# Attention value products that leave PSUM in one copy, with their halves added through DRAM, and forget gates computed with tokens on partitions

## The chip, the cores and the metric

The kernel runs on one core of a Trainium2 chip. A core has a matrix engine (TensorE, PE in the profile), three engines for elementwise work (VectorE or DVE, ScalarE or ACT, GpSimd or POOL), a queue that issues transfers (SyncE or SP) and 16 DMA engines that carry them. Each engine takes its instructions in the order of the program and waits on semaphores for the others. The metric is the device time of one execution in microseconds, the median of several runs.

## The reference

One layer of an encoder, everything in float32, for 1024 tokens of width 1024. Cut to the part that the change touches:

```python
h = rmsnorm(x, g_mix_pre)
proj = h @ w_in                       # fq fk fv | f_logit (8 columns) | cq ck cv
f_logit = proj[..., 1536:1544] + b_fgt
y_fox = forgetting_attention(fq, fk, fv, f_logit)   # 8 heads of 64
y_chk = chunked_relpos_attention(cq, ck, cv, rel_bias)  # 8 heads of 64
y = concat([rmsnorm(y_fox, g_fox_out), rmsnorm(y_chk, g_chk_out)])
x = x + rmsnorm(y @ w_out, g_mix_post)

def forgetting_attention(q, k, v, f_logit):
    logf = log_sigmoid(f_logit)
    c = cumsum(logf, axis=1)          # over the tokens, one row for each head
    logits = q @ k.T / 8 + c[query] - c[key]      # causal
    return softmax(logits) @ v
```

After that come cross-attention into 256 memory tokens (`w_mq`, `w_mk`, `w_mv`, `w_mo`) and a squared-ReLU MLP of width 4096, each between two rmsnorms and added to `x`.

## The kernel before

**Products in three parts.** TensorE multiplies in a rounded 32-bit form. To keep float32 accuracy each operand is split into a high part (a rounded copy, made by ScalarE) and a low part (the rest, made by a subtraction on VectorE or GpSimd), and each product is three matmuls into one PSUM bank: high by high, high by low, low by high (`mm3`, lines 193 to 195).

**Stages.** First the value products of four heads of each kind and the normed input are computed (up to about 57 us). Then follows the attention phase (`attention_phase`), then a second run for the output projection, cross-attention and the first half of what follows (`flow.run` a second time), then the MLP, whose order is written out by hand.

**A planner sets the order.** In the attention phase and the second run the program is written by a small planner (`Flow`). It walks a clock of its own. Generators yield steps for TensorE with a cost and a condition; at each point the first generator whose condition holds emits its step, in the order in which they are listed: value products (`value_steps`), transposes of the probabilities (`turn_steps`), scores (`score_steps`), side work such as the gates and the transposes of values and memory (`side_steps`), the inverse rms (`rstd_steps`) and at the end the projections that fill the gaps (`filler_steps`: queries, keys and values of later heads, then the memory products `mk` and `mv`). Work for the other engines is put into lists with an engine, a time from which it can run and a cost: `flow.put("V", ...)` for VectorE, `"S"` for ScalarE, `"G"` for GpSimd, `"D"` and `flow.load` for transfers on SP. Buffers are counted by tokens (`free`). `pumps` are asked at each step whether a transfer or a split can be started: weights (`stock.pump`), biases (`biases.pump`), the normed outputs of the heads (`outputs.pump`). What comes out is a fixed order on each engine.

**The heads.** There are 16 heads, taken in pairs `n` = 0 to 7 in the order of `ORDER`: two pairs of chunked heads, four pairs of forgetting heads, two pairs of chunked heads. A unit is one head and 256 queries. For a unit, scores go into PSUM, VectorE adds the bias and takes the minimum, ScalarE takes the exponential, GpSimd scales by the inverse sum, TensorE transposes the probabilities (`ptr`, line 711), ScalarE and VectorE split them (`phl`, lines 720 and 717), and TensorE multiplies them by the values (`pv`, line 754). The score matmuls (`sc`, `sf`, lines 638 and 639) need the queries `qs` and the doubled keys `kd`, `kl`, whose second half is put in place by SP transfers (line 849).

**How a unit's product leaves.** The stationary operand holds high and low values side by side, so the bank `pv` has 128 partitions: for one head the high product on 64 of them and the low product on the other 64, and each has two halves of 256 columns, from the high and the low probabilities. The result is the sum of all four. `leave` (in `value_steps`) does it in three operations and a store:

```python
flow.put("S", flow.end, 0.6, lambda: nc.scalar.activation(o2[own], pv[oth, :, :, ::step], AF.Copy), both)
# both: VectorE adds the other 64 partitions of the bank (frees the bank),
#       GpSimd adds the two halves, SP stores 64 x 256 to od[kcol][g // 2]
```

`Outputs` later loads `od` (line 1045), scales and splits it for the output projection, and sums its squares; `rstd_steps` makes the inverse rms with four small matmuls for each half of the tokens (`ssh`, line 1059). `rstd_steps(0)` (forgetting heads, both halves) is a stream of the attention phase, `rstd_steps(1)` (chunked heads) one of the second run.

**The forget gates.** The value products of the first four forgetting heads carry eight further columns, the gate logits of all eight, which ScalarE copies into `fcol` (tokens on partitions, lines 350 and 355). `forget_gates` transposes them to [8, 1024] (eight transposes, `ftr`, line 521), adds the offset, computes log-sigmoid in ten operations on eight partitions (lines 526 to 537, with two loads of ScalarE's function table), takes the running sum with a scan, and stores it to `cd` (line 538), from which each forgetting head's bias is loaded (line 576).

Of the kernel before, what the change touches and what calls it, by code (L numbers as in the profile page):

```python
# [22 lines left out]
P = 128  # L23
S = 1024
D = 1024
KC = D // P
TB = S // P
HT = 512
# [27 lines left out]
class Flow:  # L56
# [79 lines left out]
def build(ctx, tc, nc, out, t):  # L136
# [151 lines left out]
    fcol = p1.tile([P, TB, 8], F32, tag="o2", bufs=2, name="fcol")  # L288
# [52 lines left out]
    def value_leave(g, kb, ps):  # L341
# [12 lines left out]
        if g == 0:  # L354
# [8 lines left out]
            dict(s=2, tr=2, pv=2, mm=2, sp=1, p=2, klo=4, bias=2, raw=2, w=0, u4=6,  # L363
                 q=4, mp=4, pt=1, xt=2, wq=0).items()}
    seen = {}

# [146 lines left out]

    def forget_gates():

        z, e, l, u = [p1.tile([8, S], F32, tag="sp", bufs=5, name=f"f{n}") for n in "zelu"]
        parts = []
        for g in range(2):
            tr = mm_tile([8, 4, P], f"ftr{g}", "tr")
            for j in range(4):  # L520
                nc.tensor.transpose(tr[:, j, :], fcol[:, g * 4 + j, :], ident)
            parts.append(("V", 0.75, lambda g=g, tr=tr: nc.vector.tensor_scalar(
                z[:, g * HT:(g + 1) * HT], tr.rearrange("p a b -> p (a b)"), bfgt, None, op0=ALU.add)))

        parts += [
            ("V", 0.7, lambda: nc.vector.tensor_scalar(l, z, -1.0, None, op0=ALU.mult)),
            ("V", 1.2, lambda: nc.vector.tensor_tensor(l, l, z, op=ALU.min)),
            ("S", 1.1, lambda: nc.scalar.activation(e, l, AF.Exp)),
            ("V", 0.7, lambda: nc.vector.tensor_scalar(u, e, 1.0, None, op0=ALU.add)),
            ("S", 2.4, lambda: nc.scalar.activation(l, u, AF.Ln)),  # L530
            ("V", 1.3, lambda: nc.vector.scalar_tensor_tensor(e, u, 1.0, e, op0=ALU.subtract, op1=ALU.subtract)),
            ("S", 2.4, lambda: nc.scalar.activation(u, l, AF.Exp, scale=-1.0)),
            ("V", 1.2, lambda: nc.vector.tensor_tensor(e, e, u, op=ALU.mult)),
            ("V", 1.2, lambda: nc.vector.tensor_sub(e, e, l)),
            ("V", 1.3, lambda: nc.vector.scalar_tensor_tensor(e, z, 0.0, e, op0=ALU.min, op1=ALU.add)),
            ("V", 0.9, lambda: nc.vector.memset(u, 0.0)),
            ("V", 2.3, lambda: nc.vector.tensor_tensor_scan(l, e, u, 0.0, op0=ALU.add, op1=ALU.add)),
            ("D", 0.55, lambda: nc.sync.dma_start(cd, l))]

        def done(at):  # L540
            seen["gates"] = at
            for _ in range(4):
                free["sp"].give(at)

        for _ in range(2):
            free["tr"].take()
        flow.chain(flow.end, parts[:2], lambda at: [free["tr"].give(at) for _ in range(2)] and
                   flow.chain(at, parts[2:], done))
# [177 lines left out]
    def value_steps():  # L726
        landed = [all_of(("od", k), 32) for k in range(2)]
        for n, a, g in units:
            kind, pr = ORDER[n]
            h = pr * 2 + a  # L730
            own, oth = HALVES[a]
# [25 lines left out]
            def leave(pv=pv, kind=kind, nm=f"{n}{a}{g}", own=own, oth=oth, kcol=kcol, g=g, step=1 if kind == "f" else -1):  # L757
                o2 = p1.tile([P, 2, 2, P], F32, tag="o2", bufs=2, name=f"o2{nm}")

                def store(end):  # L760
                    flow.load(end, lambda: nc.sync.dma_start(
                        od[kcol][g // 2][own, (g % 2) * 256:(g % 2) * 256 + 256],
                        o2[own, 0].rearrange("p a b -> p (a b)")), landed["fc".index(kind)], 2.2)

                def both(at):
                    flow.put("V", at, 0.7, lambda: nc.vector.tensor_add(  # L766
                        o2[own], pv[own, :, :, ::step], o2[own]), lambda end: (
                        free["pv"].give(end), flow.put("G", end, 0.8, lambda: nc.gpsimd.tensor_add(  # L768
                            o2[own, 0], o2[own, 0], o2[own, 1]), store)))

                flow.put("S", flow.end, 0.6, lambda: nc.scalar.activation(o2[own], pv[oth, :, :, ::step], AF.Copy), both)  # L771
# [89 lines left out]
    def side_steps():  # L861

        yield 0.87, lambda: flow.now > 2.5 and free["tr"].ready(2)
# [128 lines left out]

    class Outputs:
# [56 lines left out]
    def rstd_steps(g):  # L1050

        for th in range(2):
            yield 0.5, lambda: there(("sq", th, g)) and free["pv"].ready()
            free["pv"].take()
            sq = parts[th, g][2]
            rs = parts["rs", th, g] = small.tile([P, 4], F32, tag="rs4", bufs=4, name=f"rs{th}{g}")
            ps = mm_tile([P, 4], f"ssh{th}{g}", "pv")
            for b in range(4):
                nc.tensor.matmul(ps[:, b:b + 1], sq[:, b * P:(b + 1) * P], o512, start=True, stop=True)
# [547 lines left out]

    stock = Stock()
    with tc.manual_schedule():
# [117 lines left out]
        nc.sync.dma_start(bfgt, t["b_fgt"])  # L1727
# [684 lines left out]
def _layout(i):  # L2412
# [10 lines left out]
    def parts(w, ranges):  # L2423
# [16 lines left out]
        "b_fgt": a(i["b_fgt"].reshape(8, 1)),  # L2440
# [26 lines left out]
```

## Time and profile before

| What | us |
|---|---|
| median of 3 runs | 1462.85 (1462.04 to 1463.18) |
| span of the profiled execution | 1459.5 |
| TensorE busy in it | 1447.7 (99%) |
| VectorE, ScalarE, GpSimd busy | 996.0, 820.7, 421.0 |

The profiled execution is told by its span, from its first to its last instruction; the time of a run has some 3 us more around it. In the page, a busy TensorE is one with a matmul in flight, and matmuls overlap, so a short pause is seen in the distance between two starts rather than as idle time. Lines such as `L766` are lines of the kernel, and names such as `o<-pv` are the tile written and the tiles read, with buffer numbers left out.

### The profile page before, as it was taken

How to read it: one execution, taken by the hardware profiler on the slowest of the kernel's cores; microseconds unless marked ns; L12 is line 12 of the kernel's file. 1: busy time of each engine (PE TensorE's matmuls, PEld its weight loads, DVE VectorE, ACT ScalarE, POOL GpSimd, SP SyncE). 2: the span in 40 equal slices, each digit the busy share in tenths (PEclk: the TensorE clock that was granted, in tenths of full speed). 3: DMA queues.
4: the chain of work that ended last, by engine and by line, in shares of the span. 5: the costliest groups of instructions: out<-in, count | busy, mean ns of one | idle time of the engine just before them, and what ended most of it. 6: DMA issues, size and time to landing. Idle time of an engine off the chain costs nothing.

```text
span 1459.5 us, 21037 instructions
## 1 busy us (share of the span) xinstructions
PE 1447.7 (99%) x7265; PEld 1222.2 (84%) x7265; DVE 996.0 (68%) x1704; ACT 820.7 (56%) x1437; POOL 421.0 (29%) x520
## 2 busy tenths in 40 slices
PE   9999999999999999999999999999999999999998
PEld 8988888888889888888788888888888888888886
DVE  6777777767668847976873687765555666655576
ACT  6567677766677836555653465545555543444442
POOL 1245456555455301521332414343322000000021
PEclk9999999999999999999999999999999999999999
DMA  7132324321325584552541637754444785445565
GB/s 276 49 95 72 83 67 140 86 82 46 95 58 161 174 314 173 187 179 86 181 138 44 200 132 260 258 196 159 159 151 161 286 318 185 140 149 190 186 246 202
DMA packets 88987, 232.17 MB, mean 159 GB/s; under 512 B 10649, under 2 KB 14753, under 8 KB 88881
## 3 DMA queue, kind: packets, MB, share of 16 engines
q1 hardware_dynamic: 88736, 230.57, 47.6%
q8 instruction: 57, 0.93, 0.3%
q14 instruction: 50, 0.40, 0.1%
q10 hardware_dynamic: 144, 0.26, 0.1%
HBM read 167.30 MB, written 55.11 MB: 152 GB/s over the span
## 4 chain that ended last, share of the span: by engine, by line
PE 96%; DVE 2%; DMA 1%; ACT 1%; issue 0%; SPq 0%; DVEq 0%; ACTq 0%
PE pv L754 4%; PE fx L194 4%; PE fx L193 4%; PE fx L195 4%; PE ptr L711 4%; PE px L194 3%; PE fy L193 3%; PE px L195 3%; PE fy L195 3%; PE px L193 3%; PE fy L194 3%; PE mq L195 2%; PE q L193 2%; PE q L195 2%; PE q L194 2%; PE yw L193 2%
## 5 line engine op out<-in xcount | busy, mean ns | idle before, releaser
L717 DVE TENSOR_TENSOR phl<-ptr,phl 128x512 fp32r<-128x512 f32 (+1 forms) x152 | 92.5, 616 | 31.5 <-ACT phl L720 30.5
L2163 ACT ACTIVATE whif<-ra 128x1024 fp32r<-128x1024 f32 x37 | 39.2, 1061 | 130.3 <-PE fy L194 62.6
L2165 DVE TENSOR_TENSOR wlof<-ra,whif 128x1024 fp32r<-128x1024 f32 x37 | 45.3, 1225 | 91.7 <-ACT whif L2163 91.7
L720 ACT ACTIVATE phl<-ptr 128x512 fp32r<-128x512 f32 (+1 forms) x152 | 79.8, 540 | 40.3 <-PE ptr L711 38.5
L2285 POOL TENSOR_SCALAR rf<-sf 128x1 f32<-128x1 f32 x7 | 7.9, 1130 | 321.7 <-ACT jf L2266 321.4
L754 PE MATMUL pv<-phl,vs 128*128 128x512 f32 (+1 forms) x304 | 85.2, 366 | 0.2 <-DVE phl L717 0.2
L193 PE MATMUL fx<-vhif,whif 128*128 128x512 f32 x168 | 65.4, 389 | 0.0
L195 PE MATMUL fx<-vhif,wlof 128*128 128x512 f32 x168 | 65.4, 389 | 0.0
L194 PE MATMUL fx<-vlof,whif 128*128 128x512 f32 x168 | 65.4, 389 | 0.0
L754 PEld LDWEIGHTS pv<-phl,vs 128*128 128x128 f32 x304 | 55.2, 188 | 11.0 <-DVE phl L717 0.7
L2050 POOL TENSOR_TENSOR sc<-wf,wf 128x512 f32<-128x512 f32 x14 | 23.1, 1652 | 141.1 <-DMA wf<-in_w_ff 122.6
L768 POOL TENSOR_TENSOR o<-o 64x256 f32<-64x256 f32 x64 | 47.8, 747 | 53.1 <-DVE o L766 29.0
L193 PE MATMUL k<-hT_hi,whik 128*128 128x512 f32 x128 | 53.6, 419 | 0.0
L766 DVE TENSOR_TENSOR o<-pv,o 64x512 f32<-64x512 f32 x64 | 44.0, 688 | 13.5 <-ACT o L771 12.1
L193 PE MATMUL q<-hT_hi,whiq 128*128 128x512 f32 x128 | 51.6, 403 | 0.0
L193 PE MATMUL mq<-h2T_hi,whimq 128*128 128x512 f32 x128 | 51.4, 401 | 0.0
L195 PE MATMUL mq<-h2T_hi,wlomq 128*128 128x512 f32 x128 | 50.2, 392 | 0.2 <-DVE wlomq L455 0.2
L195 PE MATMUL k<-hT_hi,wlok 128*128 128x512 f32 x128 | 50.3, 393 | 0.0
L194 PE MATMUL k<-hT_lo,whik 128*128 128x512 f32 x128 | 50.3, 393 | 0.0
L195 PE MATMUL q<-hT_hi,wloq 128*128 128x512 f32 x128 | 50.2, 392 | 0.0
L194 PE MATMUL q<-hT_lo,whiq 128*128 128x512 f32 x128 | 50.2, 392 | 0.0
L194 PE MATMUL mq<-h2T_lo,whimq 128*128 128x512 f32 x128 | 50.1, 392 | 0.1
(696 smaller groups left out, 5014.5 us busy)
## 6 DMA issues: line engine op xcount, KB each, us to landing
ra<-gd SPq DMA_DIRECT2D x56, 512.0 KB, 3.8
wg<-in_w_ff SPq DMA_DIRECT2D x56, 512.0 KB, 5.6
wf<-in_w_ff SPq DMA_DIRECT2D x38, 512.0 KB, 3.9
gd<-s SPq DMA_DIRECT2D x48, 256.0 KB, 2.1
wrawmq<-in_w_mq SPq DMA_DIRECT2D x16, 512.0 KB, 4.3
gd<-u SPq DMA_DIRECT2D x32, 256.0 KB, 2.2
gd<-g SPq DMA_DIRECT2D x25, 256.0 KB, 2.2
wrawq<-in_w_qk SPq DMA_DIRECT2D x8, 512.0 KB, 4.4
```

Of the source, the lines that this page charges most:

```text
L193: nc.tensor.matmul(ps, lh, rh, start=start, stop=False, skip_group_check=more)
L194: nc.tensor.matmul(ps, lh, rl, start=False, stop=False, skip_group_check=more)
L195: nc.tensor.matmul(ps, ll, rh, start=False, stop=stop, skip_group_check=more)
L711: nc.tensor.transpose(tr[:, m, :], sp[:, k * P:(k + 1) * P], ident)
L717: flow.put("V", at, 0.7, lambda: nc.vector.tensor_sub(pl[:, live, :], tr[:, live, :], f(ph[:, live, :])), done)
L720: flow.put("S", flow.end, 0.6, lambda ph=ph, tr=tr, live=live: nc.scalar.activation(ph[:, live, :], tr[:, live, :], AF.Copy), split)
L754: nc.tensor.matmul(pv[:, :, qs_, :], v, hl[:, :, hs, :], start=c == 0 and turn == 0, stop=last)
L766: flow.put("V", at, 0.7, lambda: nc.vector.tensor_add(o2[own], pv[own, :, :, ::step], o2[own]), lambda end: (free["pv"].give(end), flow.pu ...
L768: free["pv"].give(end), flow.put("G", end, 0.8, lambda: nc.gpsimd.tensor_add(o2[own, 0], o2[own, 0], o2[own, 1]), store)))
L2050: eng.tensor_sub(sc[:, k1], r0[:, k0], r1[:, k0])
L2163: nc.scalar.activation(ah, ra, AF.Copy)
L2165: nc.vector.tensor_sub(al, ra, f(ah))
```

## The change

Three things.

1. **Value products.** ScalarE copies the whole bank, all 128 partitions, in one operation, and the bank is free. GpSimd adds the two halves of 256 columns on 128 partitions. SP stores 128 x 256 to a new array in DRAM, `oh`, which for a pair of heads holds four blocks of 64 rows: high and low of the first head, low and high of the second. When the four units of a pair and half of the tokens have landed, a new pump, `fold`, loads `oh` twice, with the blocks 0 and 3 in one half of a tile and 1 and 2 in the other, adds the halves on VectorE or GpSimd (whichever the planner's lists have free sooner, `pick`), and stores the sum to `od`. `Outputs` then goes on as before. The value steps no longer use VectorE.
2. **Forget gates.** The log-sigmoid is computed on `fcol` itself, [128, 8, 8], by `gate_columns` at the start of the attention phase. The eight transposes come after it; ScalarE copies their result out of PSUM, and only the scan and the store stay on [8, 1024]. The offset `b_fgt` is loaded once for all partitions. Two of the four [8, 1024] tiles are gone, so scores start with five free buffers (`sp`) instead of one, and `side_steps` waits for two of them.
3. **Inverse rms.** The second half of `rstd_steps(0)` moves from the attention phase to the second run, ahead of `rstd_steps(1)`.

```diff
+    def behind(self, eng, at):
+        return max(self.free[eng], at) + sum(i[3] for i in self.waiting[eng])
+
+    def pick(self, at, cv, cg, call, then=None, level=0):
+
+        if self.behind("V", at) + cv + 2 < self.behind("G", at) + cg:
+            self.put("V", at, cv, lambda: call(True), then, level)
+        else:
+            self.put("G", at, cg, lambda: call(False), then, level)
...
-    bfgt = const.tile([8, 1], F32, name="bfgt")
+    bfgt = const.tile([P, 8], F32, name="bfgt")
+    gate = [const.tile([P, TB, 8], F32, name=f"gate{k}") for k in "zelu"]
...
+    oh = [[dr.tile([2 * P, HT], F32, name=f"oh{k}_{h}") for h in range(2)] for k in range(KC)]
...
-            dict(s=2, tr=2, pv=2, mm=2, sp=1, p=2, klo=4, bias=2, raw=2, w=0, u4=6,
+            dict(s=2, tr=2, pv=2, mm=2, sp=5, p=2, klo=4, bias=2, raw=2, w=0, u4=6,
...
+    def gate_columns():
+
+        z, e, l, u = gate
+        b = bfgt[:, None, :].to_broadcast([P, TB, 8])
+        flow.chain(0.0, [
+            ("V", 0.17, lambda: nc.vector.tensor_tensor(z, z, b, op=ALU.add)),
+            ("V", 0.15, lambda: nc.vector.tensor_scalar(l, z, -1.0, None, op0=ALU.mult)),
+            ("V", 0.17, lambda: nc.vector.tensor_tensor(l, l, z, op=ALU.min)),
+            ("S", 0.3, lambda: nc.scalar.activation(e, l, AF.Exp)),
+            ("V", 0.15, lambda: nc.vector.tensor_scalar(u, e, 1.0, None, op0=ALU.add)),
+            ("S", 1.6, lambda: nc.scalar.activation(l, u, AF.Ln)),
+            ("V", 0.17, lambda: nc.vector.scalar_tensor_tensor(e, u, 1.0, e, op0=ALU.subtract, op1=ALU.subtract)),
+            ("S", 1.6, lambda: nc.scalar.activation(u, l, AF.Exp, scale=-1.0)),
+            ("V", 0.17, lambda: nc.vector.tensor_tensor(e, e, u, op=ALU.mult)),
+            ("V", 0.17, lambda: nc.vector.tensor_sub(e, e, l)),
+            ("V", 0.17, lambda: nc.vector.scalar_tensor_tensor(e, z, 0.0, e, op0=ALU.min, op1=ALU.add))], mark("gate"), 1)
+
     def forget_gates():
 
-        z, e, l, u = [p1.tile([8, S], F32, tag="sp", bufs=5, name=f"f{n}") for n in "zelu"]
+        l, u = [p1.tile([8, S], F32, tag="sp", bufs=5, name=f"f{n}") for n in "lu"]
...
-                nc.tensor.transpose(tr[:, j, :], fcol[:, g * 4 + j, :], ident)
+                nc.tensor.transpose(tr[:, j, :], gate[1][:, g * 4 + j, :], ident)
+            copies.append(("S", 0.6, lambda g=g, tr=tr: nc.scalar.activation(
+                l[:, g * HT:(g + 1) * HT], tr.rearrange("p a b -> p (a b)"), AF.Copy)))
...
+        flow.chain(flow.end, [("G", 0.9, lambda: nc.gpsimd.memset(u, 0.0))] + copies, lambda at: [
+            free["tr"].give(at) for _ in range(2)] and flow.chain(at, [
+                ("V", 2.3, lambda: nc.vector.tensor_tensor_scan(l, l, u, 0.0, op0=ALU.add, op1=ALU.add)),
+                ("D", 0.55, lambda: nc.sync.dma_start(cd, l))], done))
...
                 def store(end):
                     flow.load(end, lambda: nc.sync.dma_start(
-                        od[kcol][g // 2][own, (g % 2) * 256:(g % 2) * 256 + 256],
-                        o2[own, 0].rearrange("p a b -> p (a b)")), landed["fc".index(kind)], 2.2)
+                        oh[kcol][g // 2][a * P:(a + 1) * P, (g % 2) * 256:(g % 2) * 256 + 256],
+                        o2[:, 0].rearrange("p a b -> p (a b)")), landed[kcol, g // 2], 2.2)
 
                 def both(at):
-                    flow.put("V", at, 0.7, lambda: nc.vector.tensor_add(
-                        o2[own], pv[own, :, :, ::step], o2[own]), lambda end: (
-                        free["pv"].give(end), flow.put("G", end, 0.8, lambda: nc.gpsimd.tensor_add(
-                            o2[own, 0], o2[own, 0], o2[own, 1]), store)))
-
-                flow.put("S", flow.end, 0.6, lambda: nc.scalar.activation(o2[own], pv[oth, :, :, ::step], AF.Copy), both)
+                    free["pv"].give(at)
+                    flow.put("G", at, 0.8, lambda: nc.gpsimd.tensor_add(o2[:, 0], o2[:, 0], o2[:, 1]), store)
+
+                flow.put("S", flow.end, 0.6, lambda: nc.scalar.activation(o2, pv[:, :, :, ::step], AF.Copy), both)
...
-        yield 0.87, lambda: flow.now > 2.5 and free["tr"].ready(2)
+        yield 0.87, lambda: there("gate") and free["tr"].ready(2) and free["sp"].ready(2)
...
+    folds, folded = [], [all_of(("od", g), 8) for g in range(2)]
+
+    def fold():
+
+        while folds and free["u4"].ready(3):
+            free["u4"].take()
+            fold_one(*folds.pop(0))
+
+    def fold_one(k, th):
+
+        x = u4(f"fold{k}{th}", (P, 2, HT), F32)
+
+        def out(at):
+            flow.load(at, lambda: nc.sync.dma_start(od[k][th], x[:, 0, :]), lambda end: (
+                free["u4"].give(end), folded[k // 4](end)), 2.3)
+
+        def add(v):
+            adder(v).tensor_add(x[:, 0, :], x[:, 0, :], x[:, 1, :])
+
+        both = all_of(("fold", k, th), 2, lambda at: flow.pick(at, 0.7, 1.3, add, out, 2))
+        for j, src in enumerate((oh[k][th].rearrange("(a p) n -> a p n", p=64)[::3], oh[k][th][64:192, :])):
+            flow.load(flow.now, lambda j=j, src=src: nc.sync.dma_start(x[:, j, :], src), both, 3.0, 1)
...
+    def sums_left():
+        yield from rstd_steps(0, (1,))
+        yield from rstd_steps(1)
...
-        flow.pumps += [stock.pump, biases.pump, outputs.pump]
-        flow.run([value_steps(), turn_steps(), score_steps(), side_steps(), rstd_steps(0),
+        gate_columns()
+        flow.pumps += [stock.pump, biases.pump, fold, outputs.pump]
+        flow.run([value_steps(), turn_steps(), score_steps(), side_steps(), rstd_steps(0, (0,)),
...
-        nc.sync.dma_start(bfgt, t["b_fgt"])
+        nc.sync.dma_start(bfgt, t["b_fgt"].to_broadcast([P, 8]))
...
-        flow.run([memory_out_steps(), memory_turn_steps(), memory_score_steps(), rstd_steps(1), second_rows(),
+        flow.run([memory_out_steps(), memory_turn_steps(), memory_score_steps(), sums_left(), second_rows(),
```

More of the change, by code (lines that the diff above doesn't have):

```diff
@@ L286, in bias_rows @@
         nc.sync.dma_start(rd, rrow)
-    fcol = p1.tile([P, TB, 8], F32, tag="o2", bufs=2, name="fcol")
+    fcol = gate[0]
     VPARTS = {1: ((0, 4), (4, 8)), 0: ((0, 3), (3, 6), (6, 8))}
@@ L362, in build, with adder @@
     free = {k: Tokens(flow, n) for k, n in
-            dict(s=2, tr=2, pv=2, mm=2, sp=1, p=2, klo=4, bias=2, raw=2, w=0, u4=6,
+            dict(s=2, tr=2, pv=2, mm=2, sp=5, p=2, klo=4, bias=2, raw=2, w=0, u4=6,
                  q=4, mp=4, pt=1, xt=2, wq=0).items()}
     seen = {}
+    def adder(v):
+        return nc.vector if v else nc.gpsimd
     def there(*keys):
@@ L520, in forget_gates @@
             for j in range(4):
[L521 to L538, printed above, removed]
+                nc.tensor.transpose(tr[:, j, :], gate[1][:, g * 4 + j, :], ident)
+            copies.append(("S", 0.6, lambda g=g, tr=tr: nc.scalar.activation(
+                l[:, g * HT:(g + 1) * HT], tr.rearrange("p a b -> p (a b)"), AF.Copy)))
         def done(at):
             seen["gates"] = at
-            for _ in range(4):
+            for _ in range(2):
                 free["sp"].give(at)
@@ L726, in value_steps @@
     def value_steps():
-        landed = [all_of(("od", k), 32) for k in range(2)]
+        landed = {(k, th): all_of(("oh", k, th), 4, lambda at, k=k, th=th: folds.append((k, th))) for k in range(KC) for th in range(2)}
         for n, a, g in units:
@@ L755, in value_steps, with leave @@
                 free["p"].give(flow.end)
[L757 removed]
+            def leave(pv=pv, kind=kind, nm=f"{n}{a}{g}", a=a, kcol=kcol, g=g, step=1 if kind == "f" else -1):
                 o2 = p1.tile([P, 2, 2, P], F32, tag="o2", bufs=2, name=f"o2{nm}")
@@ L861, in side_steps @@
     def side_steps():
-        yield 0.87, lambda: flow.now > 2.5 and free["tr"].ready(2)
+        yield 0.87, lambda: there("gate") and free["tr"].ready(2) and free["sp"].ready(2)
+        for _ in range(2):
+            free["sp"].take()
         forget_gates()
@@ L1048, in build, with rstd_steps @@
     outputs = Outputs()
-    def rstd_steps(g):
-        for th in range(2):
+    def rstd_steps(g, ths=(0, 1)):
+        for th in ths:
             yield 0.5, lambda: there(("sq", th, g)) and free["pv"].ready()
```

7 lines of the change are left out of this document (2 added, 5 removed).

## The prediction

> **What bounds the kernel.** I read the page first, then the busy time of each engine over the stretch that the change touches, then TensorE's own waits, then the order of its matmuls.
>
> ```profile
> span 1459.5 us, 21037 instructions
> ...
> PE 1447.7 (99%) x7265; PEld 1222.2 (84%) x7265; DVE 996.0 (68%) x1704; ACT 820.7 (56%) x1437; POOL 421.0 (29%) x520
> ...
> PE 96%; DVE 2%; DMA 1%; ACT 1%; issue 0%; SPq 0%; DVEq 0%; ACTq 0%
> ```
>
> TensorE is busy 99% of the span and makes 96% of the chain that ended last. The change removes no matmul and adds none, so it can only win back time in which TensorE stands still between 57 us (end of the opening value products) and 519 us (first output projections). That stretch, in the view by windows (start and end, length, then busy us of PE, PEld, DVE, ACT and POOL, the clock, the DMA share and GB/s):
>
> ```profile
> 57.00:519.00 462.00, 461.26 (x2548) 394.08 (x2548) 342.61 (x863) 321.42 (x632) 226.43 (x325) 1.00 0.35 98
> ```
>
> PE has 0.74 us idle here, at full clock. Its waits, by whom it waited for (the other lines of that view lie outside the stretch):
>
> ```profile
> PE sc3g L638 <- DVE mnc3g L642: 0.3, 1, 0.3
> ...
> PE sc6g L638 <- DVE mnc6g L642: 0.2, 1, 0.2
> PE mk L193 <- DVE km_lo L957: 0.2, 1, 0.2
> PE pv L754 <- DVE phl L717: 0.2, 1, 0.2
> ```
>
> This understates the loss, because matmuls overlap: the timeline gives a matmul 0.28 us and yet starts the next 0.12 us later. What counts is the distance of starts.
>
> ```profile
> 159.24 0.33 PE L639 MATMUL sc3g<-kl,qs 128*128 128x384 f32 x1
> 159.83 0.39 PE L638 MATMUL sc3g<-kd,qs 128*128 128x256 f32 x1 [0.25 <-DVE mnc3g L642]
> ...
> 455.35 0.28 PE L195 MATMUL mk<-mT_hi,wlomk 128*128 128x256 f32 x1
> 455.80 0.45 PE L638 MATMUL sc6g<-kd,qs 128*128 128x384 f32 x1 [0.17 <-DVE mnc6g L642]
> ...
> 465.40 0.60 PE L754 MATMUL pv<-phl,vs 128*128 128x512 f32 x2
> 466.16 0.39 PE L193 MATMUL mk<-mT_hi,whimk 128*128 128x256 f32 x1 [0.16 <-DVE km_lo L957]
> ...
> 486.32 0.28 PE L194 MATMUL mk<-mT_lo,whimk 128*128 128x256 f32 x1
> 486.44 0.28 PE L195 MATMUL mk<-mT_hi,wlomk 128*128 128x256 f32 x1
> 486.88 0.73 PE L754 MATMUL pv<-phl,vs 128*128 128x512 f32 x2 [0.16 <-DVE phl L717]
> ...
> 490.73 0.39 PE L195 MATMUL mv<-whimv,mT_lo 128*128 128x512 f32 x1
> 491.07 0.62 PE L754 MATMUL pv<-phl,vs 128*128 128x512 f32 x2
> ```
>
> With regular distances of 0.12 us (256 columns), 0.18 (384) and 0.23 (512), these five places lose 0.41, 0.33, 0.30, 0.32 and 0.11 us, and the first matmul after each pause takes about 0.1 more: 2.0 us. The same count over the starts of all 2548 matmuls of the stretch (nine places, from 88.46 to 491.07) gives 3.2 us. **This is the most the change can win**: 3.2 us is 0.22% of the time.
>
> **The base.** The profiled span is 1459.5; the median of the runs is 1462.85, so 3.35 us lie around the span, and I add the change to the median. Within 0.2% (2.9 us) is about what a measurement of this kernel can't tell from no change.
>
> **The value products.** Four instructions close each of 64 units:
>
> ```profile
> L771 ACT ACTIVATE o<-pv x64: 579/594/598, 95.3 to 509.3; 64x512 f32<-64x512 f32 x64
> L766 DVE TENSOR_TENSOR o<-pv,o x64: 662/689/697, 95.9 to 511.3; 64x512 f32<-64x512 f32 x64
> L768 POOL TENSOR_TENSOR o<-o x64: 724/735/1245, 96.7 to 512.3; 64x256 f32<-64x256 f32 x64
> L761 SPq DMA_DIRECT2D od<-o x64: 445/452/782, 97.4 to 513.4; - x64
> ```
>
> - The copy covers 128 partitions instead of 64 with the same 512 elements each: I take 0.59 us as before (cost follows the elements of one partition: 8x1024 takes 1.06 below). Change 0; upper bound 0.1 each, beside PE.
> - The vector add goes: 64 x 0.689 = 44.1 us off DVE's 342.6 (74% to 65% of the stretch), and the accumulator bank comes free 0.69 us sooner. All four waits above name DVE, but at 455 the chain below runs back over ACT to a DMA. I take half of the 3.2 us as won back: **-1.6**, between 0 and -3.2.
> - POOL's add covers 128x256 for 64x256: 0.735 again, at most the 1.245 maximum.
>
> **The fold through DRAM.** New are 16 times two loads of 256 KB, an add of 128x512 and a store of 256 KB; the 64 stores double to 128 KB. No such row exists; the nearest (KB, median us to landing; then the chain of waits; then POOL):
>
> ```profile
> kd<-kd SPq DMA_DIRECT2D x32, 128.0 KB, 2.3
> ...
> od<-o SPq DMA_DIRECT2D x64, 64.0 KB, 1.9
> ...
> wrawmk<-in_w_mk SPq DMA_DIRECT2D x8, 512.0 KB, 3.7
> ...
> oin<-od SPq DMA_DIRECT2D x16, 256.0 KB, 5.4
> ```
>
> ```profile
> 445.03 7.82 DMA wrawmk<-in_w_mk
> ```
>
> ```profile
> 449.94 2.55 POOL L458 TENSOR_TENSOR wlomk<-wrawmk,whimk 128x512 fp32r<-128x512 f32 x2 [0.30 <-ACT whimk L449]
> ```
>
> ```profile
> SPq L761 <- POOL o L768: 157.3, 46, 11.8
> ```
>
> POOL: in the built program it does 15 of the 16 adds, 15 x 1.27 = 19 us on 226 of 462, hidden while it idles half the time; but POOL is in order too, and a fold add whose loads are late holds up the softmax scalings queued behind it, which the `ptr` transposes wait for. SP: 48 more issues x 0.45 = 22 us. Bytes: 64 x 64 KB + 32 x 256 KB + 16 x 256 KB = 16 MB more, about 36 GB/s on 98; the DMA share goes from 0.35 to some 0.45. What costs is the queue: SP issues in order, and a fold's store waits there for POOL's add, that add for two loads, those for the last `oh` store. From the landing of that store I count 0.9 (two issues) + 2.3 to 5.4 (landing) + 1.27 (add) = 4.5 to 7.6 us in which all behind waits. Mostly nothing urgent stands there. The tight place is the last head pair: in the built order `wrawmk_1` to `_3` stand behind fold 60's store; `wrawmk_4` needs the buffer of `_1`; the second fold 61 loads and the `kd`/`kl` copies of the last key projection stand behind that, and the scores `sc6` need those copies. Between that projection and `sc6` the order has 54 matmuls of `mk`, 54 x 0.12 = 6.5 us of cover; the copies need a 0.6 split, issues of 2 and 2.3 to land, about 5. So 1.5 us is spare. I take **+0.6** for the whole fold, the middle of small slips, between 0 (loads land in 2.3 to 3) and +5.7 (below).
>
> In the Trainium skill, "DMA: Bandwidth & Descriptors", section "Anatomy of one DMA", a transfer costs about 2 us plus its bytes over 436 GB/s, which I estimate as 2.6 us for 256 KB. The 128 KB row (2.3) agrees, the 256 KB row (5.4) does not; by the page the fold's term would be 0 and the sum 0.6 lower.
>
> **The forget gates.** Eleven operations on [8,1024] become ones on [128,64], ahead of the transposes instead of behind:
>
> ```profile
> 56.82 0.39 PE L193 MATMUL q<-hT_hi,whiq 128*128 128x512 f32 x1
> ...
> 59.57 1.03 PE L521 MATMUL ftr<-ident,fcol 128*8 128x128 f32 x8
> ```
>
> ```profile
> L521 PEld LDWEIGHTS ftr<-ident,fcol x8: 84/86/87, 59.3 to 60.2; 128*8 128x8 f32 x8
> ```
>
> ```profile
> 57.30 0.17 ACT L355 ACTIVATE fcol<-v 128x8 f32<-128x8 f32 x1
> ...
> 64.63 1.06 ACT L528 ACTIVATE fe<-fl 8x1024 f32<-8x1024 f32 x1
> 65.71 1.28 ACT L530 ACT_TABLE_LOAD   x1
> ```
>
> ```profile
> 55.38 0.27 DVE L283 TENSOR_SCALAR rrow<-rsrc 8x256 f32<-8x256 f32 x1
> ...
> 57.02 0.91 DVE L356 TENSOR_TENSOR vs<-v,vs 128x256 fp32r<-128x256 f32 x2
> ...
> 62.35 1.21 DVE L527 TENSOR_TENSOR fl<-fl,fz 8x1024 f32<-8x1024 f32 x1
> ```
>
> DVE is saved eight or nine us (ten operations up to 1.21 against seven of 0.2) and ACT one, but the first reader of the gates' sums comes heads later: 0. The new wait: PE's eight transposes now need the finished gates. They stand 27 matmuls after the first `q` (12 before): 56.82 + 27 x 0.229 = 63.0, with their weight load 0.3 sooner, 62.7. The chain starts when DVE is done, 57.93. For 64 elements I take 0.2 us on DVE (0.27 at 256) and 0.22 on ACT (0.17 at 8, 1.06 at 1024): three DVE operations 0.6, exponential 0.22, table load 1.28, logarithm 0.22, table load 1.28, exponential 0.22, three DVE 0.6 = 4.4, so 62.35 and hand-overs. Just in time: **0**, at most +0.5. Behind the transposes PE has `q` matmuls queued, so a miss would cost the whole amount.
>
> The Trainium skill, "ScalarE: Activation LUTs", section "What ACT_TABLE_LOAD costs", adds a drain of 1.38 us to each load of 1.28. By it the gates would end 2.8 us later and PE would lose about 2.5, the sum then 1464.4. The row shows 1.28, starting 0.02 after the operation before it, and the drain is not seen.
>
> **Half an inverse rms moved.** Row:
>
> ```profile
> 516.98 0.95 PE L1059 MATMUL ssh<-o,sq 128*128 128x1 f32 x8
> ```
>
> In the built order these stand behind six `yw` matmuls instead of seven. Same work, same place: 0. From there on PE's order is the same in both kernels. Eight more switches between transposes and products cost about 0.02 each by their starts: **+0.1**.
>
> **Sum.** -1.6 + 0.6 + 0 + 0 + 0.1 = -0.9: 1462.85 - 0.9 = 1461.9.
>
> **Rivals.**
> A, slower: the queue behind the folds. If `wrawmk_1` lands in 7.8 us instead of 3.7, 4.1 of lateness meet 1.5 of spare: 2.6 lost before `sc6`; with fold loads at 5.4 instead of 2.3 another 3.1, so 5.7. Against -1.6 won and +0.1 that gives 1464.0 to 1467.1, about 1466. It decides from some 4.5 us of lost time in all. For it: the 7.82 row, and that SP already waits 157 us for POOL here. Against: DMA is only 35% busy, and a stall that shifts PE gives everything behind it the same slack.
> B, faster: all of the DVE waits go and nothing comes: -3.2 + 0.1, 1459.8. For it: every PE wait in the stretch names DVE. Against: 455 goes back to a DMA and ACT.
> C, the change doesn't reach TensorE at all: the same 3.2 us are lost, 1462.9; part of "same".
> D, by the table rule: 1464.4, also within 0.2%.
>
> **Chances.** Forecast with C and D 0.60 (D by itself 0.05), A 0.25, B 0.15. So faster 0.15, same 0.60, slower 0.25. The range takes B's end (1459.6, all 3.2 won) and runs to 1466.5, inside A's upper half.
>
> **What would show it.** Right: DVE about 45 to 55 us lower in the stretch, PE's sum unchanged, the distance 159.24 to 159.83 closed, no pause at the gate transposes near 63, pauses near 445 to 470 of the old size. Wrong: a pause of over 2 us before `sc6` behind `kd` copies (A), one before `ftr` (D), a wait of TensorE that goes back to a POOL add, or a pause where fold loads meet weight loads in the middle of the attention.

## The result, and the profile after

The changed kernel takes **1529.2 us** (median of 5 runs, 1528.2 to 1531.0) against 1462.5 for the kernel before: a ratio of 1.0458 with a 95% interval of 1.0446 to 1.0471, or 66.7 us slower. The forecast was 1461.9, with 1466.5 as its upper end.

The page of the changed kernel first: its span, its engines, and the head of the chain that ended last.

```profile
span 1526.8 us, 21041 instructions
...
PE 1466.7 (96%) x7265; PEld 1233.2 (81%) x7265; DVE 953.3 (62%) x1639; ACT 814.3 (53%) x1439; POOL 434.7 (28%) x536
...
PE 38%; DVE 1%; issue 0%; ACT 0%; DVEq 0%; ACTq 0%
```

TensorE has the same 7265 matmuls, but is busy for 96% of the span instead of 99%. The chain's shares add up to only 39% of the span: it was followed back from the end to 927 us and no further, so it says nothing about the stretch that the change touches. The same stretch of work, from the first query projection to the first output projection, now ends at 572 instead of 515 (the view by windows, columns as before):

```profile
57.00:572.00 515.00, 472.56 (x2528) 399.78 (x2528) 294.07 (x792) 313.53 (x632) 238.10 (x338) 0.97 0.39 117
```

PE stands idle 42.4 of 515 us, where it was 0.74 of 458 (57 to 515 in the kernel before), and the granted clock is 0.97 instead of 1.00. VectorE is 44.6 us lighter for the same work (294.07 after 338.64), about as forecast, and that won nothing. TensorE's waits, in the view of waits of the changed kernel:

```profile
PE ptr L730 <- POOL spc6g L673: 9.4, 1, 9.4
PE ssh L1100 <- DVE sq L1060: 5.9, 1, 5.9
PE ptr L730 <- POOL spc4g L673: 5.5, 1, 5.5
...
PE sf6g L657 <- DMA kd<-kd: 4.7, 1, 4.7
PE sf1g L657 <- DVE mnf1g L661: 3.6, 1, 3.6
...
PE ftr L553 <- DVE gatee L544: 2.0, 1, 2.0
```

A few long pauses, each behind another engine. Counted by the distances of starts from 57 to 655 us, some 22 places lose about 51 us (4 places and 1.4 us before), and some 110 small ones lose about 15 (18 and 2.1). Most of these small ones stand behind the long ones, as below.

What is late is told by the view of transfers (KB, median us to landing), the transfers and waits of the tile `fold` (its last line mixes loads and stores), and SP's waits:

```profile
fold<-oh SPq DMA_DIRECT2D x32, 256.0 KB, 7.9
...
od<-fold SPq DMA_DIRECT2D x16, 256.0 KB, 9.2
```

```profile
L1032 SPq DMA_DIRECT2D fold<-oh x32: 424/504/3892, 174.9 to 576.0; - x32
...
  POOL fold L1028: 73.8, 12
  DVE fold L1028: 3.0, 1
...
DMA to landing us min/median/max: 7.7/8.5/10.1
```

```profile
SPq L1024 <- POOL fold L1028: 54.6, 10, 10.1
```

The fold's loads land in 7.9 us in the median, not in 2.3 to 5.4. One of their issues held SP for 3.9 us. GpSimd waited 73.8 us for them, twelve times, with the rest of its work behind, and SP waited 54.6 us for GpSimd's adds before it could issue the fold's stores. How that reaches TensorE shows at its longest pause (timeline of the changed kernel; the bracket is the idle time before the instruction and what ended it):

```profile
498.21 1.06 SPq L1032 DMA_DIRECT2D fold<-oh  x2
...
509.09 1.26 POOL L1028 TENSOR_TENSOR fold<-fold 128x512 f32<-128x512 f32 x1 [12.23 <-DMA fold<-oh]
...
512.77 2.05 POOL L673 TENSOR_SCALAR spc6g<-spc6g,smc6g 128x128 f32<-128x128 f32 x4
...
513.65 0.90 PE L730 MATMUL ptr<-ident,spc6g 128*128 128x128 f32 x3 [9.38 <-POOL spc6g L673]
...
515.63 0.41 PE L204 MATMUL mk<-mT_lo,whimk 128*128 128x256 f32 x1
515.84 0.41 PE L205 MATMUL mk<-mT_hi,wlomk 128*128 128x256 f32 x1
```

The scores of `sc6g` had been ready since 504, but their scaling stands on GpSimd behind the fold's add and two weight splits, and the add waits 12.2 us for its loads. TensorE stands for 9.4 us. When it starts again, matmuls of 256 columns follow each other every 0.21 us instead of 0.12 for some 3 us, and the granted clock from 513.6 to 517.0 us is 0.50: a long pause is paid for again at a lower clock, and most of the small losses counted above are of this kind. The Trainium skill, "TensorE: Matmul & The Clock Gate", in "Part 1: The HAM clock gate (the "warmup" mystery)", says that an array which has been idle runs at half its clock until it has been busy for about 3.4 us; this trace agrees.

### The profile page after: what moved, and what is told of

Read it like the earlier page. It is cut to its first block, busy times and chain, and to the rows that moved or that the text cites. A ratio compares the mean times of both kernels' runs of the same rounds, so it can differ in the third digit from the quotient of the medians.

```text
span 1526.8 us, 21041 instructions
## 1 busy us (share of the span) xinstructions
PE 1466.7 (96%) x7265; PEld 1233.2 (81%) x7265; DVE 953.3 (62%) x1639; ACT 814.3 (53%) x1439; POOL 434.7 (28%) x536
## 5 line engine op out<-in xcount | busy, mean ns | idle before, releaser
L785 POOL TENSOR_TENSOR o<-o 128x256 f32<-128x256 f32 x64 | 49.4, 772 | 55.8 <-ACT o L787 55.4
L203 PE MATMUL yw<-whiwo,yT_hi 128*128 128x512 f32 x128 | 51.2, 400 | 0.6 <-ACT yw L1239 0.6
L205 PE MATMUL yw<-whiwo,yT_lo 128*128 128x512 f32 x128 | 50.6, 395 | 0.0
L204 PE MATMUL yw<-wlowo,yT_hi 128*128 128x512 f32 x128 | 50.6, 395 | 0.0
```

The lines of the kernel that those rows point to most:

```text
L203: nc.tensor.matmul(ps, lh, rh, start=start, stop=False, skip_group_check=more)
L204: nc.tensor.matmul(ps, lh, rl, start=False, stop=False, skip_group_check=more)
L205: nc.tensor.matmul(ps, ll, rh, start=False, stop=stop, skip_group_check=more)
L785: flow.put("G", at, 0.8, lambda: nc.gpsimd.tensor_add(o2[:, 0], o2[:, 0], o2[:, 1]), store)
```

## Experiments

Every run was timed against the kernel before on the same chip, whose median was 1461.3 to 1461.8 us there. Differences below are against it.

**The pattern of one load, taken out.** The fold's first load takes blocks 0 and 3 of `oh`, two runs of 64 rows with a gap of 128 between them. In e1 it reads 128 rows in a row; nothing else moves.

```diff
-        for j, src in enumerate((oh[k][th].rearrange("(a p) n -> a p n", p=64)[::3], oh[k][th][64:192, :])):
+        for j, src in enumerate((oh[k][th][0:128, :], oh[k][th][64:192, :])):
```

> The changed kernel with one thing different: the first of the two loads of a fold reads the 128 contiguous rows 0 to 127 of its array instead of the two separate blocks of 64 rows 0 to 63 and 192 to 255. Instructions, sizes, waits and order stay the same; half of the sums come out of the wrong rows, so the output is not the reference's. Theory (pattern): the load whose outermost step counts only two blocks is carried by few of the 16 DMA engines; that makes the fold loads land in 7.9 us instead of about 3, fills the rings of those engines for all transfers behind, and holds POOL's and SP's queues. Then the loads land in 2.5 to 4 us here, POOL's waits for fold loads fall from 77 us to under 15, and the time to 1462 to 1469. Rival (traffic): it is the extra hop through DRAM, 16 MB more and 48 more issues in one queue, whatever the pattern; then loads stay above 6 us and the time above 1510.

In e2 the same bytes come by two loads of 64 rows:

```diff
+        for rows, j, src in ((slice(0, 64), 0, oh[k][th][0:64, :]), (slice(64, 128), 0, oh[k][th][192:256, :]),
+                             (slice(0, 128), 1, oh[k][th][64:192, :])):
```

> The changed kernel, computing the same, with the load of two separate blocks issued as two loads of 64 contiguous rows each (three loads to a fold, 16 more issues). Theory (pattern): as with contiguous rows, 1462 to 1469, the fold's loads landing in 2.5 to 4 us. Rival (traffic): 16 issues more, so no better than 1529, rather above it.

e1: **1475.7 us** (+14.1, ratio 1.0096, interval 1.0081 to 1.0111). e2: **1473.5** (+11.9, 1.0080, 1.0065 to 1.0095). The tile `fold` in e1:

```profile
L1032 SPq DMA_DIRECT2D fold<-oh x32: 319/383/601, 176.4 to 522.5; - x32
...
  POOL fold L1028: 8.0, 5
...
DMA to landing us min/median/max: 2.0/3.0/8.3
```

Same bytes, same places on SP, same order: the loads land in 3.0 instead of 7.9 us in the median, none of their issues takes longer than 0.6, GpSimd waits 8 us instead of 74, and 53 to 55 of the 66.7 us are gone. The pattern is the main cause. The times lie 6.7 and 4.5 us above the expected 1462 to 1469, so the pattern is not the whole of it. (In e1 half of the sums come from the wrong rows; e2 computes what the change computes.)

**One part at a time.** e3 is the kernel before with part 2 alone, e4 with part 1 alone (two-block load as in the change), e12 with part 3 alone (the two lines with `rstd_steps(0, (0,))` and `sums_left`).

> The kernel before with the second part of the change alone: forget gates with tokens on partitions. In the changed kernel TensorE stands 2 us before the gates' transposes, where two VectorE operations on 64 elements take 1.2 us each instead of 0.2. Theory: that pause of about 2 us comes back whole, 1463.5 to 1465.5 (about +2). Rival: a later slack swallows it, 1462 to 1463.

> The kernel before with the first part of the change alone: value products in one copy, folded through DRAM, two-block load as in the change. Theory (pattern and traffic alike): this part makes nearly all of the loss, 1522 to 1530, TensorE's pauses again in front of folds. Rival: the loss needs the gates too, since they let the scores start with five buffers; then under 1500.

> Part 3 alone: half an inverse rms goes into the next run, nothing else changed. The prediction's step says 0: 1461 to 1463 us. If the moved half costs by itself, 1464 us or more.

e3: **1471.7 us** (+10.1, 1.0073, 1.0056 to 1.0089). e4: **1555.4** (+93.8, 1.0640, 1.0624 to 1.0655). e12: **1462.2** (1.0004, 0.9995 to 1.0013), no difference. So the fold alone is 27 us worse than the whole change, and the gates, forecast at 0, cost ten. For e3 and e4 both expectations failed, the theory's and the rival's. The parts don't add up, which already says that more is at work than two durations; why the fold alone is worse stays open.

**The fold with good loads, alone.** e5 is part 1 alone with the loads of e2.

> Part 1 alone on the kernel before (gates and inverse rms as before), with the two-block load issued as two loads of 64 rows each. If the slow pattern is the whole price of the fold, nothing but small waits is left: 1460 to 1465 us. If a fold that stands in line on SP, GpSimd and VectorE costs by itself, whatever its loads take, it stays well above: 1469 to 1480 us.

**1466.8 us** (+5.0, 1.0037, 1.0023 to 1.0051), 1.8 us above the first expectation and below the second: from 94 us to 5 by the form of one load.

**The slow load without a reader.** e8 is the kernel before with two loads added at each of the sixteen places, into a spare tile that nothing reads; e11 is the same with rows in a row.

```diff
+        rows = t["w_out"][0:256, 0:HT]
+        for j, src in enumerate((rows.rearrange("(a p) n -> a p n", p=64)[::3], rows[64:192, :])):   # e11: rows[0:128, :]
+            flow.load(flow.now, lambda j=j, src=src: nc.sync.dma_start(x[:, j, :], src), both, 3.0, 1)
```

> The kernel before with two added loads of 256 KB for each of the sixteen fold places: one with the two-block pattern, one of 128 rows in a row, both from a weight in DRAM into a spare tile that no engine reads; no fold, no halves by DRAM, gates as before. If the slow pattern hurts by holding up the other loads of the queue, the time rises by 15 to 50 us and other loads land late. If it hurts only through the engines that wait for it in their order, the time stays within 5 us of the kernel before.

> As the two-block loads on the kernel before, with the first load reading 128 rows in a row instead: same bytes, same number of loads, same places. If the pattern is the cause, 1461 to 1465 us. If it is the added bytes or the places on SP's queue, 1480 to 1492 us as with the two-block loads.

e8: **1490.4 us** (+28.6, 1.0197, 1.0183 to 1.0211). e11: **1463.5** (+1.7, 1.0014, 1.0005 to 1.0023). TensorE, VectorE, ScalarE and GpSimd have the same order in both. So the pattern costs 27 us with nobody waiting for its data. The timeline of e8 shows how:

```profile
190.08 5.20 SPq L576 DMA_DIRECT2D biasf<-cd  x1
...
207.26 0.54 POOL L600 TENSOR_SCALAR_AFFINE_SELECT biasf<-biasf 128x128 f32<-128x128 f32 x2 [11.33 <-DMA biasf<-cd]
...
208.38 0.58 PE L638 MATMUL sf1g<-kd,qs 128*128 128x256 f32 x1 [5.89 <-DVE mnf1g L642]
...
463.48 6.06 SPq L1008 DMA_DIRECT2D fold<-in_w_out  x2
...
469.69 0.52 PE L638 MATMUL sc6g<-kd,qs 128*128 128x256 f32 x1 [2.32 <-DMA kd<-kd]
```

A load of a bias, issued behind a two-block load, keeps SP for 5.2 us and lands some 17 us after its start, where the same load takes 4.5 in the kernel before; GpSimd, VectorE and then TensorE wait for it. At 463 the two issues of the fold take SP 6.1 us. The key copies `kd`, issued at 458.6 and 460.4 behind two loads of the fold, have not landed for `sc6g` until 469.7, where such a copy lands in 2.3 in the kernel before. In e11 no issue of the added loads takes longer than 1.2 us; in e8 one takes 4.2. A slow load thus holds up SP itself and what is queued behind it. The other half of the price in the changed kernel would then be the readers', which wait in their engines' order; that half is a subtraction between two kernels, and no run measures it by itself.

**The gates.** e9 tells the planner what the first three VectorE steps took (next section), so that the transposes stand later in TensorE's order. e7 takes two of the score tokens away again: three are free until the gates' transposes (not one, as its expectation says), one until the gates are stored, five from then on.

```diff
-            ("V", 0.17, lambda: nc.vector.tensor_tensor(z, z, b, op=ALU.add)),              # e9: 0.5
-            ("V", 0.15, lambda: nc.vector.tensor_scalar(l, z, -1.0, None, op0=ALU.mult)),   # e9: 1.2
-            ("V", 0.17, lambda: nc.vector.tensor_tensor(l, l, z, op=ALU.min)),              # e9: 1.25
```

> Part 2 alone, with the planner told what the first three VectorE steps of the gate chain took (0.5, 1.2 and 1.25 us for 0.17, 0.15 and 0.17), so that the gates' transposes stand some 2.5 us later in TensorE's order. If the wait before the transposes and what it shifts is the whole price of the gates, 1461 to 1465 us and no wait before ftr. If most of the price is in how the planner's other steps fall against each other, the 2 us before ftr go and the rest stays or moves: 1467 to 1473 us.

> Part 2 alone, with the score tokens as in the kernel before: one until the gates are done, five from then on. If the early tokens are what costs (the planner lets more scores run ahead, and VectorE and ScalarE fall behind), 1462 to 1466 us with only the 2 us before the gates' transposes left. If the wait itself and what it shifts costs, 1470 to 1473 us as with the gates alone.

e9: **1470.6 us** (+8.8, 1.0064, 1.0051 to 1.0077), and the wait before `ftr` is gone. e7: **1473.3** (+11.5, 1.0078, 1.0066 to 1.0091), with the same waits as e3: the tokens are not it. A further run, e6, has the kernel of e3 once more, part 2 alone; its expectation was written for the edit of e9 and is answered there:

> Part 2 alone, with the planner told what the first three VectorE steps of the gate chain took on the chip (0.5, 1.2 and 1.25 us for 0.17, 0.15 and 0.17). If the ten microseconds of the gates come from the wait of TensorE before the gates' transposes and what that wait shifts, the transposes now stand some 2 us later in TensorE's order and the time is 1462 to 1466 us. If they come from the changed order of the steps (more score tokens early), the time stays at 1469 to 1473 us.

**1473.5 us** (+11.7, 1.0079, 1.0066 to 1.0093). Two runs of one kernel thus lie 1.8 us apart, so that e9's gain on them, 1 to 3 us, is little more than this spread.

e10 makes the negation and the minimum one instruction:

```diff
-            ("V", 0.15, lambda: nc.vector.tensor_scalar(l, z, -1.0, None, op0=ALU.mult)),
-            ("V", 0.17, lambda: nc.vector.tensor_tensor(l, l, z, op=ALU.min)),
+            ("V", 0.17, lambda: nc.vector.scalar_tensor_tensor(l, z, -1.0, z, op0=ALU.mult, op1=ALU.min)),
```

> Part 2 alone, with the negation and the minimum of the gate chain as one VectorE instruction. If VectorE's small instructions are held at 1.2 us each by GpSimd's splits, one instruction less shortens TensorE's wait before the gates' transposes by 1.2 us, from 2.0 to 0.8. If the instructions are simply as slow as their work, the wait shrinks by at most the 0.2 us that their later fellows take. Time 1468 to 1472 us either way, because the later waits stay.

**1471.8 us** (+10.0, 1.0070, 1.0057 to 1.0084). Its timeline:

```profile
58.24 2.54 POOL L473 TENSOR_TENSOR wlok<-wrawk,whik 128x512 fp32r<-128x512 f32 x2
58.39 1.21 DVE L535 SCALAR_TENSOR_TENSOR gatel<-gatez 128x64 f32<-128x64 f32 x1
...
59.93 0.90 DVE L537 TENSOR_SCALAR gateu<-gatee 128x64 f32<-128x64 f32 x1 [0.32 <-ACT gatee L536]
60.86 0.23 DVE L539 SCALAR_TENSOR_TENSOR gatee<-gateu,gatee 128x64 f32<-128x64 f32 x1
...
63.87 1.04 PE L552 MATMUL ftr<-ident,gatee 128*8 128x128 f32 x8 [0.75 <-DVE gatee L543]
```

One instruction less takes 1.24 us off TensorE's wait (1.99 to 0.75), which is too little to show in the time, and the one that moved up into GpSimd's subtraction now takes 0.90 where it took 0.20. Each of them ends when a subtraction of GpSimd ends (58.24 + 2.54 = 60.78), and the next takes 0.23.

**The order alone.** e13 and e14 are the kernel before with one number of the planner changed, the time from which the gates' transposes may stand in the plan. No instruction is new, none is gone.

```diff
-        yield 0.87, lambda: flow.now > 2.5 and free["tr"].ready(2)
+        yield 0.87, lambda: flow.now > 3.5 and free["tr"].ready(2)    # e14: 8.0
```

> The kernel before with one number of the planner changed: the gates' transposes may stand in the plan from 3.5 us on in place of 2.5. Every instruction is one of the kernel before; only their order on the queues differs from there on. If the order that the planner happens to find carries the price that the gates' new costs left (some 8 us), another order of the same work is also slower: 1466 to 1473 us. If the order does not matter and the new gates' instructions do, 1461 to 1464 us.

> As the one before, with 8.0 in place of 2.5. By the order's theory again some microseconds slower, with waits at other places: 1464 to 1472 us. By the other, 1461 to 1464 us.

e13: **1474.4 us** (+13.1, 1.0089, 1.0075 to 1.0103), 1.4 us more than the order's theory allowed. e14: **1471.7** (+10.4, 1.0072, 1.0059 to 1.0084), with waits at other places, the longest (1.6 us) before `ptr` of `spc0g`. TensorE's longest waits in e13, and then in e9:

```profile
PE sc2g L638 <- DVE mnc2g L642: 1.7, 2, 1.3
PE sf4g L638 <- DMA kd<-kd: 1.5, 1, 1.5
PE pv L754 <- DVE phl L717: 1.2, 1, 1.2
PE sf3g L638 <- DVE mnf3g L642: 0.9, 1, 0.9
```

```profile
PE sf4g L657 <- DMA kd<-kd: 1.7, 1, 1.7
PE sc2g L657 <- DVE mnc2g L661: 1.2, 2, 0.9
PE pv L773 <- DVE phl L736: 1.2, 1, 1.2
PE sf3g L657 <- DVE mnf3g L661: 0.9, 1, 0.9
```

These are the same waits at the same tiles, once with the old gates and once with the new ones. The traces show why: aligned by the tiles that they write and read, 96% of the first 3000 matmuls of e13 match those of e9, and only some 70% of either match the kernel before. It is nearly one order, found twice. One microsecond in the plan is enough to fall into it; the order of the kernel before is one in which nearly nothing meets.

**The transposes held longer.** e15 is part 2 alone, e16 the whole change with the loads of e2, both with the transposes held in the plan until 12 us (`flow.now > 12.0 and there("gate")`).

> Part 2 alone, with the gates' transposes held in the plan until 12 us, a third order for the same gates. By the order's theory the wait before ftr is gone and the other waits differ from those of the gates alone, the time anywhere from 1463 to 1474 us. If the gates' instructions themselves cost (DVE and ACT steps that later work waits for), the same waits stand at the same steps: 1468 to 1471 us.

> The changed kernel with the two-block load in two halves and the gates' transposes held until 12 us in the plan. The two known causes, the load pattern and the wait before the gates, are both out. By the order's theory what is left is some microseconds of scattered waits: 1464 to 1473 us. If the two causes were all, 1460 to 1463 us, which would be as fast as the kernel before or faster.

e15: **1469.8 us** (+8.5, 1.0056, 1.0043 to 1.0069), with the waits of e9. Its time lies in both expected ranges, and the same waits at the same steps are what the second expectation names, against the order's theory. But it was not the third order that it was meant to be: 99.7% of its first 3000 matmuls match those of e9, so it can't tell the two apart. That the waits need no new instruction rests on e13. e16: **1469.4** (+8.1, 1.0052, 1.0039 to 1.0066), in nearly the order of e2 (99.7%), without the wait before `ftr`. Its two longest waits (in the profiled run, the slowest of the five with 1472.0):

```profile
PE ssh L1101 <- DVE sq L1061: 3.4, 1, 3.4
PE ptr L730 <- POOL spc4g L673: 1.9, 2, 1.6
```

Those are the fold's: a scaling behind a fold's add on GpSimd, and squares that VectorE is late with. The four waits of e13 and e9 are not among e16's, nor among those of e1 and e2. No version tried is faster than the kernel before. What the remaining 5 us of e5 are made of, the order or the fold's adds in GpSimd's queue, was not told apart.

## Why the prediction was wrong

- **The bound**, no more than 3.2 us to win, is contradicted by no run. Nothing of it was won.
- **Value products, -1.6.** The durations held, and VectorE lost its 64 adds. The instructions on the tile `o` in the changed kernel (ns min, median, max):

```profile
L787 ACT ACTIVATE o<-pv x64: 574/597/603, 97.0 to 566.6; 128x512 f32<-128x512 f32 x64
L785 POOL TENSOR_TENSOR o<-o x64: 725/738/1702, 97.7 to 567.3; 128x256 f32<-128x256 f32 x64
```

  The four short waits that stood behind VectorE were replaced by longer ones. What this term is worth by itself no run shows; e5, which has it together with a fold with good loads, is 5.0 us slower.
- **Fold, +0.6, at most +5.7: the step that failed.** It bounded the load by `kd` (2.3 us for 128 KB) and `oin` (5.4 for 256 KB), as if only bytes mattered. Neither row has the form of the new load, two blocks of rows, and there was no row that had. The fold's loads, the two-block ones and those in rows behind them, took 7.9 us in the median; with the same bytes in rows they took 3.0 (e1), inside these bounds. I also let the upper bound come from waits that the trace of before already had; a load that slows its queue for all others has no row there either. The mechanism that costs most stands in the prediction word for word ("a fold add whose loads are late holds up the softmax scalings queued behind it") but was given no price of its own, because the loads were taken to be nearly on time. Measured: 53 to 55 us by e1 and e2, of which about 27 come without any reader (e8 against e11).
- A rule against the load was there to be found. The Trainium skill, "DMA: Bandwidth & Descriptors", "Why a DMA increments its semaphore by 16 and not by 1", says that a transfer is spread over the largest number of engines, up to 16, that divides the slowest dimension of both its sides. Here that is 2. With the 436 GB/s for 16 engines and the fixed 2 us that the Trainium skill gives on the same page, two engines carry 54.5 GB/s, and an estimate from it is 2 + 262,144 bytes / 54.5 GB/s = 6.8 us. (The Trainium skill fits that fixed part, on which the prediction's 2.6 us rests too, to transfers issued from GpSimd; here SP issues them.) The landing times agree in size (7.9 in the median). That it was two engines shows in the view by windows, first of the changed kernel and then of e1, each shortly behind the same three issues of fold loads, two of which have two blocks in the changed kernel:

```profile
177.90:182.90 5.00, 5.00 (x29) 4.20 (x28) 4.14 (x14) 3.38 (x9) 2.16 (x5) 1.00 0.13 50
```

```profile
177.80:179.80 2.00, 2.00 (x12) 1.74 (x11) 1.21 (x5) 1.64 (x4) 1.67 (x2) 1.00 0.94 341
```

  The DMA share, the mean busy share of the 16 engines, is 0.13 at 50 GB/s, which is two of 16, against 0.94 at 341 GB/s.
- **Gates, 0, at most +0.5.** "At most" failed. The chain was forecast to end at 62.35 with 0.2 us for each VectorE step (of which there are eight, not seven) and ended at 65.16. The timeline of the changed kernel:

```profile
58.34 2.53 POOL L473 TENSOR_TENSOR wlok<-wrawk,whik 128x512 fp32r<-128x512 f32 x2
58.49 1.18 DVE L535 TENSOR_SCALAR gatel<-gatez 128x64 f32<-128x64 f32 x1
59.71 1.24 DVE L536 TENSOR_TENSOR gatel<-gatel,gatez 128x64 f32<-128x64 f32 x1
...
61.26 1.28 ACT L539 ACT_TABLE_LOAD   x1
...
62.55 0.26 ACT L539 ACTIVATE gatel<-gateu 128x64 f32<-128x64 f32 x1
...
64.93 0.23 DVE L544 SCALAR_TENSOR_TENSOR gatee<-gatez,gatee 128x64 f32<-128x64 f32 x1
...
65.21 1.04 PE L553 MATMUL ftr<-ident,gatee 128*8 128x128 f32 x8 [1.99 <-DVE gatee L544]
```

  Two small VectorE steps take 1.2 us each beside GpSimd's subtractions, and TensorE waits 2.0 us. That loss was foreseen in its place, for rival D's reason; but the table load costs 1.28 and the next operation starts 0.01 after it, so D's reason is refuted. The Trainium skill, "SBUF — State Buffer", "SBUF: two separate sides", says that VectorE and GpSimd share a pair of ports, and that a GpSimd instruction that has the pair keeps a VectorE one with two inputs in SBUF or in a two-port mode waiting to its end; e10 agrees with that. The other 8 us of the gates alone are the order (e9, e13), a term that the sum didn't have. In the whole change the order is another one, and what the gates cost there beyond the 2.0 us was not measured.
- **Inverse rms, 0:** right (e12).
- **Switches, +0.1:** the order was counted only for what it changes in TensorE's own switching. That a changed cost or time in the plan can give another order, in which steps meet that didn't meet before, was worth 8 to 13 us in the runs with the gates alone and in e13 and e14.
- **Rival A** had the queue behind the folds and the sign, and a chance of 0.25. Its place was only near: the longest pause stands in the last head pair, but before the transposes of `spc6g` and behind a fold's add on GpSimd, and the wait for `kd` (4.7 us) stands before `sf6g`, in the middle of the attention; in e8 there is a wait of 2.3 us for `kd` before `sc6g`. Its price of 5.7 was about a tenth of the real one, by the same load time.

In sum: 53 to 55 us from the form of one load, about 2 from the wait before `ftr`, and the remaining 10 to 12 from the order and the fold's waits together, which were not told apart.

## What to carry to other kernels

Look at the form of a new transfer as closely as at its bytes: an outer dimension of two in one load made the fold's loads land in 7.9 us instead of about 3, and SP and the queues behind it paid; two loads of 64 rows each did the same work without that. Where the order is written by a planner and the kernel has almost no idle time left, price any change of its costs as a new order; moving one number by 1 us with no instruction changed cost 13 us here. An engine in order turns a late load into a wait for all that stands behind, so ask of each new wait not what it delays but what is queued behind it.

## What the runs showed of the hardware

- With one of the two loads of 256 KB in two blocks of 64 rows, both landed in 7.9 us in the median (the view doesn't part them); with both in rows, in 2.9 to 5.8 (e11, median 3.2). While two-block loads alone were in flight, the DMA share was 0.13 (50 GB/s); with rows it was 0.94 (341 GB/s, e1). Other transfers behind it were late too, and a single issue of these loads held SP for up to 4.2 us in e8, against 1.2 in e11.
- VectorE's steps of 64 elements took 1.2 us beside a GpSimd subtraction and 0.2 without. Later, in e16, an add of 128x512 took 1.78 us beside the fold's adds on GpSimd, where it takes 0.68 alone. Of the two adds the first, beside other work of VectorE, took 1.80 and the second 1.26, where 1.29 is their median:

```profile
522.19 3.02 POOL L1028 TENSOR_TENSOR fold<-fold 128x512 f32<-128x512 f32 x2 [5.69 <-DMA fold<-oh]
...
523.97 1.78 DVE L1061 TENSOR_TENSOR sq<-sq,oin 128x512 f32<-128x512 f32 x1
```

- Behind a pause of TensorE of 9.4 us, matmuls ran at 0.21 us instead of 0.12 for some 3 us, at a granted clock of 0.50; by the distances of starts all such slow starts together cost 13 to 14 of the 67 us.
